# Down projection of a decoder trunk step: residual additions two at a time behind each operand split in VectorE's order, and the splits of a product's last three steps held for its copies

## The chip, the core and the metric

The kernel runs on one core of one Trainium2 chip. The metric is the device time of one execution in microseconds (us). The engines are TensorE (PE in the profile, its weight loads PEld), VectorE (DVE), ScalarE (ACT), GpSimd (POOL) and SyncE (SP), which here issues DMA transfers.

## The reference

One step of a hybrid decoder trunk of one layer: a combined input projection, a gated delta rule, sliding-window attention with sinks, an output projection, and a gated feed-forward block, for 1024 prompt rows and 8 single-token samples. All data is float32. The part that the change touches is the last line of the feed-forward block, the down projection with its gate and residual:

```python
h2 = _rmsnorm(x, lp['norm2_w']) * (1 + sc2) + sh2
gate = h2 @ lp['w_ffn_gate']
up = h2 @ lp['w_ffn_up']
...
gc = _causal_dwconv(gate_ext, lp['ffn_conv_w'], L) + lp['ffn_conv_b']
x = x + gt2 * ((jax.nn.silu(gc) * up) @ lp['w_ffn_down'])
...
y_prompt = _rmsnorm(xp, final_norm_w)
```

Here `w_ffn_down` is 2816 x 1024.

## The kernel before, in words

**Products.** `ffn_down` computes this matrix product as seven products of half-size blocks (a Strassen scheme), named 1 to 7, in the order 5, 3, 4, 7, 1, 2, 6. The inner dimension of each product is taken in G = 11 steps, numbered on through all products: product 5 has the steps 0 to 10, product 3 has 11 to 21, product 4 has 22 to 32, product 7 has 33 to 43, and so on. Products 5 and 3 accumulate in the same eight PSUM banks (a chain), and so do 4 and 7; products 1 and 2 are chains of their own, and product 6 is done behind the loop.

**Operands.** For each step `fetch` loads a block of weights (256 KB) and a block of activations `xd` (258 KB) into a raw buffer. Products 3, 4, 7, 1 and 6 need the sum or the difference of two weight blocks: a second block goes to a buffer `ws`, and GpSimd adds it (L1755). Then `part` splits the raw operand into a high and a low part: ScalarE writes the high part (`hi`, L129), VectorE subtracts it (`lo`, L130). The split operands have 13 rooms (`tags`). The raw buffers are only five: three named `raw` and one, `bmh0`, that holds two steps; a load waits for the split that read its buffer last, five steps earlier.

**Matmuls, copies, additions.** `step` makes 24 matmuls per step: eight banks (p, j), and three (high x high, high x low, low x high; L180 to L182) for each. After a product's eleventh step, `take` has ScalarE copy each bank (L1786) to one of eight slots of `self.copies`. Each copy is put on the list `waiting`, once or twice, as its product belongs to one or two quarters of the output (`home`: two for 5, 3, 1 and 2; one for 4, 7 and 6). `add` takes one off the list and adds it, times the gate, to the residual tiles `x1` on VectorE: one scalar_tensor_tensor (L1472), and for the sample rows two small ones of 8 columns (L1476, L1477). The first homes of all eight copies come before the second homes, so slot 0 is read by the first and by the ninth addition where there are two homes. The next copy into a slot waits for the additions that read it.

**What sets the order.** The order in which each engine gets its instructions is set by a scheduler that plays the program with estimated costs; a semaphore then links what depends on each other. An instruction made inside `issue_after(x)` is placed behind x. `fetch_to(s + 13)` asks, at step s, for loads and splits of up to thirteen steps ahead; with its second argument false it only loads, and the splits are held. `part` puts splits behind the last copy asked for so far (`self.took`). In the kernel before, splits are held in the last six steps of a chain's last product only, and the additions, two per step in the steps 2 to 9 of the next product, are bound by nothing but their operands.

Of the kernel before, what the change touches and what calls it, by code (L numbers as in the profile page):

```python
# [9 lines left out]
F32 = mybir.dt.float32  # L10
# [3 lines left out]
ALU = mybir.AluOpType  # L14
# [50 lines left out]
class Step:  # L65
# [61 lines left out]
    def split(self, hi, lo, x, eng=None):  # L127

        self.nc.scalar.activation(hi, x, AF.Copy)  # L129
        (eng or self.nc.vector).tensor_tensor(lo, x, hi.bitcast(F32), op=ALU.subtract)  # L130

    def load_split(self, pool, shape, src, tags, bufs, raws, home=None, raw=None):

# [1592 lines left out]
    def ffn_down(self, pool, psum):  # L1726

        nc, I = self.nc, self.I
        G, n = FT // 2, NT // 2
        tags = ("bmh2", "bml0", "bml2", "bmh1", "pk2", "bml1", "pk3", "pk6", "pk4", "pk0", "pk5", "pk1", "bmh3")  # L1730
# [7 lines left out]
        ready, loaded, waiting = {}, {}, ([], [])  # L1738
# [3 lines left out]
        def fetch(s):  # L1742
            i, g = steps[s]
            if s % 5 == 3:
                ready["raw"] = self.t(self.bm, [P, KC, QW], "bmh0").rearrange("p k n -> p (k n)")
            raw = self.t(self.pw, [P, n + 512], "raw", bufs=3) if s % 5 < 3 else \
                ready["raw"][:, (s % 5 - 3) * 1040:(s % 5 - 3) * 1040 + n + 512]
            at, *src = made[i]
            src = [x if type(x) is not tuple else
                   I["w_ffn_down"][0][(2 * g + x[0]) * P:(2 * g + x[0] + 1) * P, 512 * x[1]:512 * x[1] + 512] for x in src]  # L1750
            nc.sync.dma_start(raw[:, n:], src[0])
            if len(src) > 1:
                other = self.t(self.pw, [P, 512], "ws", bufs=3)
                nc.sync.dma_start(other, src[1])
                nc.gpsimd.tensor_tensor(raw[:, n:], raw[:, n:], other, op=src[2])  # L1755
            nc.sync.dma_start(raw[:, :n], self.xd[at, g])
            loaded[s] = raw

        def part(s):
            room = self.room(tags[s % len(tags)], [P, KC * QW])  # L1760
            hi, lo = room[:, :n + 512], room[:, n + 512:2 * (n + 512)]
            with ExitStack() as after:
                for ins in (self.last_up, self.last_copy) if 5 <= s < len(tags) else (self.took,) if s >= len(tags) and self.took else ():
                    after.enter_context(self.tc.issue_after(ins.ins))
                self.split(hi, lo, loaded.pop(s))
            ready[s] = hi, lo
            if s == 5:
                less.append(self.t(pool, [P, KC, 9], "less"))
                nc.gpsimd.tensor_scalar(less[0], self.mT[:, 40:48, :], -1.0, None, op0=ALU.mult)
                for j in (2, 3, 4):  # L1770
                    self.x1[j] = self.t(pool, [P, NT], f"x1_{j}")
            if 18 <= s < 24:
                nc.sync.dma_start(self.x1[s - 16], self.x1d[s - 16])

        def step(s, ps, p, j, first, last, kw):
            hi, lo = ready[s]
            x, w = slice(256 * p, 256 * p + 256 + 4 * p), slice(n + j * P, n + j * P + P)
            self.mm3(ps, hi[:, w], lo[:, w], hi[:, x], lo[:, x], first, last, **kw)

        def add(ps, p, j, d, q, sign):  # L1780
            self.add_gated(2 * p + q, ps, j + 4 * d, 40, self.mT[:, 40:48, :] if sign > 0 else less[0])

        def take(ps, i, p, j):
            self.turn = (self.turn + 1) % KC
            r = self.copies[:, self.turn, :256 + 4 * p]
            self.took = nc.scalar.copy(r, ps)  # L1786
            for k, h in enumerate(home[i]):
                waiting[k].append((r, p, j, *h))
# [3 lines left out]
        s = begun = done = 0  # L1792

        def fetch_to(n, split=True):
            nonlocal begun, done
            n = min(n, len(steps))
            while done < n if split else begun < n and begun < done + 4 + (begun % 5 != 3):
                if begun == done or not split:
                    fetch(begun)
                    begun += 1  # L1800
                else:
                    part(done)
                    done += 1

        for c in chains[:-1]:
            ps = {(p, j): self.t(pl, [P, 512], tag, bufs=k)[:, :256 + 4 * p] for (p, j), (pl, tag, k) in zip(order, banks)}
            for i in c:
                for g in range(G):
                    fetch_to(s + len(tags), i != c[-1] or g < G - 6)
                    for p, j in order:  # L1810
                        step(s, ps[p, j], p, j, g == 0 and i == c[0], g == G - 1, {"skip_group_check": True} if i != c[0] else {})
                        if g == G - 1:
                            take(ps[p, j], i, p, j)
                    if g in range(2, 10):
                        for _ in range(2):
                            if waiting[0] or waiting[1]:
                                add(*(waiting[0] or waiting[1]).pop(0))
                    s += 1
        for x in waiting[0] + waiting[1]:
            add(*x)  # L1820
# [251 lines left out]
```

## Time and profile before

| | us |
|---|---|
| three runs | 2094.0, 2088.38, 2085.28 |
| median | 2088.38 |
| profiled execution, span from the first to the last instruction (no other time is given for it) | 2084.4 |
| TensorE busy in it | 2012.7 (97%) |
| VectorE busy | 1347.8 (65%) |
| ScalarE busy | 900.2 (43%) |
| GpSimd busy | 520.2 (25%) |
| mean granted TensorE clock | 0.991 |

The span is 0.9 us under the fastest run and 4.0 under the median. The down projection's TensorE work lies between some 1837 us and the end. A row of a timeline gives the start, the duration, the engine, the line, the operation, and what it writes and reads; the square bracket at its end is the idle time ahead of it on its engine and what ended it. Names are those of the buffers' tags: split operands have names such as pk, bmh and bml, PSUM banks are mm, wv, wy and nr, copies are bml as well (written in L1786, read in L1472), and x is the residual.

### The profile page before, as it was taken

To read this page: it belongs to the slowest core of one execution; us is meant where nothing else is said; L and a number is where in the kernel's file an instruction comes from. 1 tells how busy PE (TensorE), PEld (TensorE's weight loads), DVE (VectorE), ACT (ScalarE), POOL (GpSimd) and SP (SyncE) were. 2 spreads that over 40 slices of the span, in tenths; PEclk is the share of its full clock that TensorE was granted. 3 is DMA by queue.
4 is the path that set the end of the run, shared out by engine and by line. 5 is a ranking of instruction groups with operands and counts; after the bars stand their busy time and mean duration, and the time that the engine had idled before them with its cause. 6 is when DMAs were issued, how large, how long until landed. Compare 5 with 4: busy or idle time off the path is not lost.

```text
span 2084.4 us, 41297 instructions
## 1 busy us (share of the span) xinstructions
PE 2012.7 (97%) x16245; PEld 1910.2 (92%) x16245; DVE 1347.8 (65%) x2714; ACT 900.2 (43%) x2233; POOL 520.2 (25%) x594
## 2 busy tenths in 40 slices
PE   7999998999999999989989999999999999999897
PEld 4987877799999999989989999999999999999897
DVE  5755768473655647656544675578876776767756
ACT  4664545433344243432342542354444444534443
POOL 2000000121321221201111000005575466446421
PEclk9999999999999999999999999999999999999999
DMA  8256443331332322312275855323333333488862
GB/s 300 62 144 210 135 167 116 117 94 51 80 80 61 73 72 52 89 42 62 63 223 172 285 186 163 112 63 97 105 91 112 102 92 112 136 305 266 291 215 94
DMA packets 301887, 275.75 MB, mean 132 GB/s; under 512 B 59730, under 2 KB 248111, under 8 KB 301676
## 3 DMA queue, kind: packets, MB, share of 16 engines
q1 hardware_dynamic: 295642, 252.14, 39.6%
q0 software_dynamic: 5552, 20.37, 2.8%
q8 instruction: 127, 2.08, 0.4%
q14 instruction: 68, 0.56, 0.1%
q10 hardware_dynamic: 498, 0.61, 0.1%
HBM read 212.93 MB, written 62.51 MB: 132 GB/s over the span
## 4 chain that ended last, share of the span: by engine, by line
PE 83%; DVE 5%; DMA 5%; ACT 3%; issue 1%; SPq 1%; POOL 1%; DVEq 0%; POOLq 0%; ACTq 0%
PE mm L180 19%; PE mm L181 18%; PE mm L182 18%; PE wv L180 3%; PE wv L182 3%; PE wv L181 3%; PE wy L182 2%; PE wy L180 2%; PE wy L181 2%; PE pv L652 1%; PE pt L190 1%; PE tp L190 1%; DVE x L1472 1%; PE mm L264 1%; PE rc L954 1%
## 5 line engine op out<-in xcount | busy, mean ns | idle before, releaser
L180 PE MATMUL mm<-b1h,wh 128*128 128x384 f32 (+1 forms) x1520 | 496.9, 328 | 3.7 <-ACT gt L1294 1.6
L181 PE MATMUL mm<-b1l,wh 128*128 128x384 f32 (+1 forms) x1520 | 489.3, 323 | 0.0
L182 PE MATMUL mm<-b1h,wl 128*128 128x384 f32 (+1 forms) x1520 | 488.0, 323 | 0.3 <-DVE wl L130 0.3
L180 PEld LDWEIGHTS mm<-b1h,wh 128*128 128x128 f32 x1520 | 286.7, 189 | 12.4 <-issue 4.6
L181 PEld LDWEIGHTS mm<-b1l,wh 128*128 128x128 f32 x1520 | 287.1, 189 | 4.4 <-issue 3.1
L182 PEld LDWEIGHTS mm<-b1h,wl 128*128 128x128 f32 x1520 | 286.3, 189 | 3.9 <-issue 2.8
L129 ACT ACTIVATE wh<-raw 128x1024 fp32r<-128x1024 f32 x83 | 87.0, 1049 | 122.4 <-PE mm L181 70.2
L130 DVE TENSOR_TENSOR wl<-raw,wh 128x1024 fp32r<-128x1024 f32 x82 | 101.0, 1233 | 57.2 <-ACT wh L129 55.1
L181 PE MATMUL mm<-pk,w 128*128 128x260 f32 (+1 forms) x440 | 124.8, 284 | 1.1 <-DVE pk L130 1.1
L180 PE MATMUL mm<-pk,w 128*128 128x260 f32 (+1 forms) x440 | 124.8, 284 | 0.0
L182 PE MATMUL mm<-pk,w 128*128 128x260 f32 (+1 forms) x440 | 124.5, 283 | 0.0
L130 DVE TENSOR_TENSOR w<-ws,w 128x512 fp32r<-128x512 f32 x88 | 78.0, 886 | 36.9 <-ACT w L129 36.7
L1626 ACT COPY bml<-mm 128x256 f32<-128x256 f32 (+1 forms) x132 | 48.9, 371 | 100.6 <-PE mm L182 96.7
L180 PE MATMUL mm<-bmh,w 128*128 128x260 f32 (+1 forms) x320 | 90.3, 282 | 0.0
L182 PE MATMUL mm<-bmh,w 128*128 128x260 f32 (+1 forms) x320 | 90.1, 282 | 0.0
L1681 DVE SCALAR_TENSOR_TENSOR fa<-fz,fcw,fa 128x512 f32<-128x512 f32 x88 | 75.2, 874 | 18.2 <-ACT fa L1679 17.9
L180 PE MATMUL mm<-b2h,wh 128*128 128x384 f32 (+1 forms) x256 | 83.2, 328 | 2.9 <-ACT wh L129 2.8
L181 PEld LDWEIGHTS mm<-pk,w 128*128 128x128 f32 x440 | 83.2, 189 | 1.3 <-DVE pk L130 1.3
L181 PE MATMUL mm<-b2l,wh 128*128 128x384 f32 (+1 forms) x256 | 83.6, 327 | 0.4 <-DVE b2l L130 0.4
L180 PEld LDWEIGHTS mm<-pk,w 128*128 128x128 f32 x440 | 83.2, 189 | 0.2 <-ACT bml L1626 0.2
L182 PEld LDWEIGHTS mm<-pk,w 128*128 128x128 f32 x440 | 83.4, 190 | 0.0
L182 PE MATMUL mm<-b2h,wl 128*128 128x384 f32 (+1 forms) x256 | 82.8, 326 | 0.0
(645 smaller groups left out, 5886.2 us busy)
## 6 DMA issues: line engine op xcount, KB each, us to landing
raw<-in_w_in_dram SPq DMA_DIRECT2D x59, 512.0 KB
ws<-in_w_ffn_down_dram SPq DMA_DIRECT2D x55, 256.0 KB
raw<-xd SPq DMA_DIRECT2D x47, 258.0 KB
raw<-in_w_ffn_down_dram SPq DMA_DIRECT2D x47, 256.0 KB
raw<-in_w_ffn_gate_dram SPq DMA_DIRECT2D x22, 512.0 KB
raw<-in_w_ffn_up_dram SPq DMA_DIRECT2D x22, 512.0 KB
qst<-in_w_mod_dram SPq DMA_DIRECT2D x16, 512.0 KB
raw<-in_w_mod_dram SPq DMA_DIRECT2D x16, 512.0 KB
```

The costliest lines, as they stand in the source:

```text
L129: self.nc.scalar.activation(hi, x, AF.Copy)
L130: (eng or self.nc.vector).tensor_tensor(lo, x, hi.bitcast(F32), op=ALU.subtract)
L180: mm(ps, whi, xhi, start=first, stop=False, **kw)
L181: mm(ps, whi, xlo, start=False, stop=False, **kw)
L182: self.last_mm = mm(ps, wlo, xhi, start=False, stop=last, **kw).ins
L190: self.nc.tensor.transpose(out, in_, self.ident[:p, :p])
L264: nc.tensor.matmul(ps[32 * j:32 * j + 32], self.cT[:, k0 + j, :], ws[j // 2][:, j % 2, :], start=k0 == 0, stop=k0 > 0)
L652: nc.tensor.matmul(pv[64 * r:64 * r + 64], V[:, n - back, ch], ps[:, r::2, :], start=back == 0, stop=back == (n > 0))
L954: yield step(nc.tensor.matmul(ds, kd[:, n, :], s, start=True, stop=True))
L1472: nc.vector.scalar_tensor_tensor(x[:, :np_], ps[:, :np_], by[:, j, 8:9], x[:, :np_], op0=ALU.mult, op1=ALU.add)
L1626: self.last_copy = nc.scalar.copy(r[p, i], x[p])
L1681: nc.vector.scalar_tensor_tensor(ai[:, c:e], zi[:, j + c:j + e], col(j), ai[:, c:e], op0=ALU.mult, op1=ALU.add)
```

## The change

`split` keeps its VectorE instruction as `self.lo`. In `ffn_down` the splits are now also held in the last three steps of a chain's first product (5 and 4). And the additions of a step, two at most, are placed behind the last split that was asked for, which is that of twelve steps ahead where splits are not held, and otherwise the last one that was not held.

```diff
@@ -127,7 +127,7 @@
     def split(self, hi, lo, x, eng=None):
 
         self.nc.scalar.activation(hi, x, AF.Copy)
-        (eng or self.nc.vector).tensor_tensor(lo, x, hi.bitcast(F32), op=ALU.subtract)
+        self.lo = (eng or self.nc.vector).tensor_tensor(lo, x, hi.bitcast(F32), op=ALU.subtract)
...
@@ -1806,15 +1806,16 @@
             for i in c:
                 for g in range(G):
-                    fetch_to(s + len(tags), i != c[-1] or g < G - 6)
+                    fetch_to(s + len(tags), g < (G - 6 if i == c[-1] else G - 3))
                     for p, j in order:
                         step(s, ps[p, j], p, j, g == 0 and i == c[0], g == G - 1, {"skip_group_check": True} if i != c[0] else {})
                         if g == G - 1:
                             take(ps[p, j], i, p, j)
                     if g in range(2, 10):
-                        for _ in range(2):
-                            if waiting[0] or waiting[1]:
-                                add(*(waiting[0] or waiting[1]).pop(0))
+                        with self.tc.issue_after(self.lo.ins):
+                            for _ in range(2):
+                                if waiting[0] or waiting[1]:
+                                    add(*(waiting[0] or waiting[1]).pop(0))
                     s += 1
```

No instruction is added or removed on any engine; what changes is the order. Lines behind L1815 have a number higher by one in the changed kernel.

VectorE where product 4 takes over from product 3, before. The rows that write bmh_2861, bmh_2864 and bml_2867 are the splits of the steps 25, 26 and 27, and the L1472 rows with `mT` are additions of product 3's copies:

```order
L130 TENSOR_TENSOR bmh_2861_21547<-raw_21541,bmh_2861_21547 128x1028
L130 TENSOR_TENSOR bmh_2864_21582<-raw_21576,bmh_2864_21582 128x1028
L1472 SCALAR_TENSOR_TENSOR x_4_2810_21062<-bml_2334_15602,mT,x_4_2810_21062 128x256 x2
L1472 SCALAR_TENSOR_TENSOR x_4_2810_21062<-bml_2334_15602,mT,x_4_2810_21062 128x260
L1472 SCALAR_TENSOR_TENSOR x_4_2810_21062<-bml_2334_15602,mT,x_4_2810_21062 128x252
L1476 TENSOR_TENSOR gtmp_22120<-bml_2334_15602,mT 128x8
L1472 SCALAR_TENSOR_TENSOR x_5_2785_21012<-bml_2334_15602,mT,x_5_2785_21012 128x256 x2
L1472 SCALAR_TENSOR_TENSOR x_5_2785_21012<-bml_2334_15602,mT,x_5_2785_21012 128x260
L1472 SCALAR_TENSOR_TENSOR x_5_2785_21012<-bml_2334_15602,mT,x_5_2785_21012 128x252
L1476 TENSOR_TENSOR gtmp_22158<-bml_2334_15602,mT 128x8
L1477 TENSOR_TENSOR x_4_2810_21062<-x_4_2810_21062,gtmp_22120 128x8
```

The same place in the changed kernel. The L1472 rows with `less` are additions of product 5's copies, which before stood between the splits of the steps 15 and 18:

```order
L130 TENSOR_TENSOR bmh_2861_21547<-raw_21541,bmh_2861_21547 128x1028
L1472 SCALAR_TENSOR_TENSOR x_0_2332_15597<-bml_2334_15602,less_21058,x_0_2332_15597 128x256
L1472 SCALAR_TENSOR_TENSOR x_0_2332_15597<-bml_2334_15602,less_21058,x_0_2332_15597 128x260
L130 TENSOR_TENSOR bmh_2864_21582<-raw_21576,bmh_2864_21582 128x1028
L1472 SCALAR_TENSOR_TENSOR x_1_2333_15598<-bml_2334_15602,less_21058,x_1_2333_15598 128x256
L1472 SCALAR_TENSOR_TENSOR x_1_2333_15598<-bml_2334_15602,less_21058,x_1_2333_15598 128x260
L130 TENSOR_TENSOR bml_2867_21617<-raw_21611,bml_2867_21617 128x1028
L1472 SCALAR_TENSOR_TENSOR x_2_2808_21060<-bml_2334_15602,less_21058,x_2_2808_21060 128x256
L1472 SCALAR_TENSOR_TENSOR x_2_2808_21060<-bml_2334_15602,less_21058,x_2_2808_21060 128x260
L1472 SCALAR_TENSOR_TENSOR x_3_2809_21061<-bml_2334_15602,less_21058,x_3_2809_21061 128x256
L1472 SCALAR_TENSOR_TENSOR x_3_2809_21061<-bml_2334_15602,less_21058,x_3_2809_21061 128x260
L1472 SCALAR_TENSOR_TENSOR x_4_2810_21062<-bml_2334_15602,less_21058,x_4_2810_21062 128x256
```

Product 5's additions moved from behind its copies to here, two behind each split up to step 27 and the other twelve behind that one; the last row shown, into x_4, is the ninth. Product 3's additions, which stood here, went on to the place shown last.

ScalarE at the same place; bml_2867 is again the split of step 27, and the L1786 rows are the copies of product 3's banks:

```order
 L129 ACTIVATE bmh_2864_21582<-raw_21576 128x1028
+L129 ACTIVATE bml_2867_21617<-raw_21611 128x1028
 L1786 COPY bml_2334_15602<-mm_21015 128x256
 L1786 COPY bml_2334_15602<-wv_21016 128x260
 L1786 COPY bml_2334_15602<-wy_21017 128x256
 L1786 COPY bml_2334_15602<-mm_21018 128x260
-L129 ACTIVATE bml_2867_21617<-raw_21611 128x1028
 L1786 COPY bml_2334_15602<-wv_21019 128x256
+L1786 COPY bml_2334_15602<-mm_21021 128x256
```

Step 27's split moved from the middle of the copies to ahead of them.

VectorE where product 7 takes over from product 4; bmh_2912, bml_2915 and bml_2919 are the splits of the steps 39, 40 and 41, and the L1472 rows are additions of product 3's copies:

```order
 L130 TENSOR_TENSOR bmh_2912_22056<-bmh_2908_22016,bmh_2912_22056 128x1028
+L1472 SCALAR_TENSOR_TENSOR x_7_2787_21014<-bml_2334_15602,mT,x_7_2787_21014 128x256
+L1472 SCALAR_TENSOR_TENSOR x_7_2787_21014<-bml_2334_15602,mT,x_7_2787_21014 128x260
+L130 TENSOR_TENSOR bml_2915_22091<-raw_22085,bml_2915_22091 128x1028
+L1472 SCALAR_TENSOR_TENSOR x_4_2810_21062<-bml_2334_15602,mT,x_4_2810_21062 128x256
+L1472 SCALAR_TENSOR_TENSOR x_4_2810_21062<-bml_2334_15602,mT,x_4_2810_21062 128x252
+L1476 TENSOR_TENSOR gtmp_22120<-bml_2334_15602,mT 128x8
+L1477 TENSOR_TENSOR x_4_2810_21062<-x_4_2810_21062,gtmp_22120 128x8
+L130 TENSOR_TENSOR bml_2919_22129<-raw_22123,bml_2919_22129 128x1028
+L1472 SCALAR_TENSOR_TENSOR x_5_2785_21012<-bml_2334_15602,mT,x_5_2785_21012 128x256
+L1472 SCALAR_TENSOR_TENSOR x_5_2785_21012<-bml_2334_15602,mT,x_5_2785_21012 128x252
+L1476 TENSOR_TENSOR gtmp_22158<-bml_2334_15602,mT 128x8
```

Product 3's additions now stand two behind each split from step 36 on. The ninth, the first into x_4 here, is behind step 40's split, and those into x_5 are behind step 41's. On ScalarE the splits of the steps 40 and 41 likewise moved from among product 4's eight copies and from behind them to ahead of the first.

## The prediction

> **What bounds the kernel now.** I read the page's first part, then TensorE's waits, then stretches of the down projection, then each engine's rows around the two places where one product takes over from another.
>
> ```profile
> PE 2012.7 (97%) x16245; PEld 1910.2 (92%) x16245; DVE 1347.8 (65%) x2714; ACT 900.2 (43%) x2233; POOL 520.2 (25%) x594
> ...
> PE mm L180 <- ACT bml L1786: 5.6, 1, 5.6
> ...
> 1862.00:1894.00 32.00, 32.00 (x271) 32.00 (x270) 25.01 (x34) 13.11 (x18) 18.68 (x11) 1.00 0.91 323
> 1894.00:1934.00 40.00, 34.44 (x288) 34.23 (x287) 33.04 (x38) 17.48 (x25) 21.40 (x15) 0.98 0.83 275
> 1934.00:1962.00 28.00, 28.00 (x215) 28.00 (x216) 22.05 (x27) 12.06 (x16) 15.62 (x10) 0.90 0.88 291
> 1929.37:1932.78 3.41, 0.00 (x0) 0.00 (x0) 1.79 (x2) 0.99 (x2) 1.94 (x2) 1.00 1.02 376
> 1932.78:1936.19 3.41, 2.47 (x11) 2.47 (x12) 2.75 (x2) 3.41 (x10) 2.49 (x2) 0.50 1.03 387
> 1936.19:1939.61 3.42, 3.42 (x18) 3.42 (x17) 3.39 (x6) 2.39 (x4) 1.95 (x2) 0.50 0.94 279
> 1939.61:1943.02 3.41, 3.41 (x31) 3.41 (x30) 3.41 (x6) 1.06 (x1) 1.99 (x2) 1.00 0.88 278
> ```
>
> TensorE is busy for 97% of the span, and in the down projection it waits once, 5.6 us, for a copy that ScalarE makes. The windows give busy time of TensorE, its weight loads, VectorE, ScalarE and GpSimd, then granted clock and DMA share. Only 1894 to 1934 has an idle TensorE; VectorE is busy for 33.0 of its 40 us. After the idle stretch the granted clock is 0.50 for two windows.
>
> ```profile
> 1896.42 0.28 PE L182 MATMUL nr<-pk 128*128 128x260 f32 x1
> 1896.54 0.28 PE L180 MATMUL mm<-pk 128*128 128x256 f32 x1
> ...
> 1927.76 0.28 PE L181 MATMUL nr<-pk 128*128 128x260 f32 x1
> 1927.88 0.28 PE L182 MATMUL nr<-pk 128*128 128x260 f32 x1
> 1933.72 0.58 PE L180 MATMUL mm<-pk 128*128 128x256 f32 x1 [5.56 <-ACT bml L1786]
> ...
> 1934.32 0.41 PE L182 MATMUL mm<-pk 128*128 128x256 f32 x1
> 1934.53 0.41 PE L180 MATMUL mm<-pk 128*128 128x256 f32 x1
> ```
>
> Product 4 starts at 1896.54 with no idle. Product 7 starts at 1933.72 after 5.56 us. Matmuls follow at 0.12 us, and at 0.21 under the halved clock. From 1933.72 to 1939.61 the half clock covers 5.89 us, in which 0.12/0.21 of the work is done: about 2.6 us lost. So the stall of before costs 5.56 + 2.6 = **8.2 us**, and that is all this part of the kernel can give back: 0.39% of the time.
>
> ```profile
> 1910.97 1.21 DVE bmh L130
> ...
> 1912.59 1.31 SPq L1756
> 1913.89 0.05 issue
> 1913.94 4.54 DMA bmh<-in_w_ffn_down_dram
> ...
> 1918.62 1.29 POOL bmh L1755
> 1919.91 0.02 issue
> 1919.93 1.08 ACT pk L129
> 1921.01 0.02 issue
> 1921.04 2.20 DVE pk L130
> ...
> 1933.32 0.36 ACT bml L1786
> 1933.68 0.04 issue
> 1933.72 0.58 PE mm L180
> ```
>
> The chain of waits tells why. Five raw operands fit. Step 34's load goes out when VectorE's split of step 29 frees its room (1910.97), lands 4.54 us later, is summed on GpSimd, split by ScalarE and by VectorE. From there the splits follow each other up to the copy at 1933.32, which stands behind step 39's split on ScalarE.
>
> **The change part by part.** No instruction is added or taken away; three things move. (1) The 16 additions of product 5's copies, and the 16 of product 3's, leave the place right behind the copies; they stand two by two behind the splits of the steps 25 to 27 and 36 to 41. (2) ScalarE's splits of 27, 40 and 41 go ahead of the copies. (3) The splits of 28 to 32 stay behind all eight copies, as before. The eight copy slots link these: a copy may be made only when the additions that read its slot eleven steps earlier are done, and slot 0 is read by the first and the ninth.
>
> ```profile
> L1472 DVE SCALAR_TENSOR_TENSOR x<-bml,mT,x 128x256 f32<-128x256 f32 (+2 forms) x16 | 11.8, 798 | 0.0
> L1472 DVE SCALAR_TENSOR_TENSOR x<-bml,less,x 128x256 f32<-128x256 f32 (+2 forms) x16 | 9.4, 645 | 3.6 <-ACT bml L1786 3.6
> ...
> 1863.21 2.35 DVE L1472 SCALAR_TENSOR_TENSOR x<-bml,less,x 128x256 f32<-128x256 f32 x4 [3.62 <-ACT bml L1786]
> 1865.56 0.87 DVE L1472 SCALAR_TENSOR_TENSOR x<-bml,less,x 128x256 f32<-128x256 f32 x2
> 1891.78 1.23 DVE L130 TENSOR_TENSOR bmh<-raw,bmh 128x1028 fp32r<-128x1028 f32 x1
> 1902.25 1.22 DVE L130 TENSOR_TENSOR bml<-raw,bml 128x1028 fp32r<-128x1028 f32 x1
> 1923.27 6.66 DVE L130 TENSOR_TENSOR pk<-raw,pk 128x1028 fp32r<-128x1028 f32 x3
> 1933.44 1.46 DVE L130 TENSOR_TENSOR bmh<-bmh,bmh 128x1028 fp32r<-128x1028 f32 x1 [2.25 <-ACT bmh L129]
> ...
> 1896.22 1.10 ACT L129 ACTIVATE bml<-raw 128x1028 fp32r<-128x1028 f32 x1
> ...
> 1894.47 1.30 POOL L1755 TENSOR_TENSOR raw<-raw,ws 128x512 f32<-128x512 f32 x1 [0.30 <-DMA ws<-in_w_ffn_down_dram]
> ```
>
> An addition costs 11.8/16 = 0.74 us or 9.4/16 = 0.59 us, and 0.87/2 = 0.43 where GpSimd does not sum beside it. The splits it now follows have a GpSimd sum each, as in the 11.8 row, so I take 0.74; 0.43 and 1.1 (a pair of additions, 0.87, that lets a sum of 1.29 pass first: 2.16/2) are the ends.
>
> The Trainium skill ("SBUF — State Buffer", section "Who interferes with whom") says that a VectorE instruction with both inputs in SBUF and a GpSimd instruction that reads it exclude each other for a whole instruction. The splits of 2.20 us beside sums, against 1.22 alone, agree; taken for every pair of additions it would give 1.1 instead of 0.74 and is one of the rivals below.
>
> *Where product 4 takes over (1896.54).* Product 5's additions were made from 1863.21 on. Now the first two wait for step 25's split, which VectorE made at 1891.78, because only five operands are loaded ahead whatever the order asks. The ninth stands behind step 27's split and four others. Step 27's sum ends at 1894.47 + 1.30 = 1895.8; ScalarE 1.10, VectorE 1.22: 1898.1; five additions of 0.74: 1901.8; the copy and its signal 0.40: 1902.2. That is a new stall of 5.7 us, and by the only stall of that length, 2.6 us of clock: product 4 ends 8.3 us later, at 1928.16 + 8.3 = 1936.5. With 0.43 per addition, and with splits made earlier by the idle 9% of the DMA in 1862 to 1894 (2.9 us), the stall is 1.2 us without a clock loss; the upper end, 1.1 per addition, is 7.5 + 2.6.
>
> *Where product 7 takes over (1933.72).* Here the end is set, since both products are waited for. Seven more additions and eight small ones (0.08 apart) end at 1901.8 + 5.2 + 0.6 = 1907.6; the last copy, 1908.0. Then ScalarE's split of 28, 1.1, and VectorE's of 28 and 29, 1.2 each: 1911.4, where before has 1910.97 + 1.21 = 1912.2. That is 0.8 us earlier, so step 34's split, done at 1921.04 + 2.20 = 1923.2, is done at 1922.4. From there before needs (1934.9 - 1923.2)/5 = 2.33 us per split up to step 39, with VectorE idle for only 2.25 us. Six splits to step 40 are 14.0 us, and the eight additions now among them 5.9; half of the idle, 1.1, hides some: 1922.4 + 14.0 + 5.9 - 1.1 = 1941.2. The ninth addition 0.74, the copy 0.40: TensorE goes on at **1942.3** instead of 1933.72, 5.8 us after product 4's end. In the new order 13 matmuls on two banks stand ahead of the third bank: 2.8 us at half clock, to 1945.1. The third slot's addition stands behind step 41's split: 1941.2 + 1.5 + 0.15 + 2.2 + 0.74 + 0.40 = 1946.2, 1.1 us more. The clock then costs 2.6, as before.
>
> **Sum:** 8.3 for the first stall, 5.8 + 1.1 + 2.6 = 9.5 for the second, less 8.2 that before pays: **+9.6 us**, 2084.4 to 2094.0 of span. The same from the other side: product 7 goes on 1942.3 + 1.1 - 1933.72 = 9.7 later. So the first stall's size hardly matters unless the second goes. At the later takeovers (7 to 1, 1 to 2, 2 to 6) additions also move behind later splits; TensorE does not wait there now, and products 1 and 2 load less (DMA share 0.75, 0.56), so I put nothing on them:
>
> ```profile
> 1962.00:1996.00 34.00, 34.00 (x288) 34.00 (x288) 18.35 (x19) 13.90 (x19) 6.56 (x5) 1.00 0.75 253
> 1996.00:2028.00 32.00, 32.00 (x271) 32.00 (x270) 22.20 (x35) 14.04 (x19) 11.74 (x8) 1.00 0.56 183
> ```
>
> If that cover, VectorE's 15.6 and 9.8 idle us, were gone, a third stall would cost some 5 us. The profiled span is 4.0 us under the median of the runs, 2088.38, so I forecast 2088.4 + 9.6 = **2098.0 us**.
>
> **Rivals.** *Not slower: the additions hide.* What spaces the splits from 34 to 40 may be the loads (DMA share 1.02 and 1.03 in two windows) and not VectorE; then additions cost nothing there. At 0.43 each, the first burst ends 4.5 us before the old one (1898.1 + 12 x 0.43 + 0.6 + 0.4 + 1.1 + 2.4 = 1907.7 against 1912.2). Step 40's split ends at 1923.2 - 4.5 + 14.0 = 1932.7 and TensorE could go on at 1933.5, while product 4, with the first stall at 3.9 + 2.6, ends at 1934.7: no second stall. Net 6.5 - 8.2 = -1.7: 2086.7. It decides once the additions among the splits cost under some 1.5 us together. For it: the DMA share; against it: VectorE's 6.66 us for three splits without a gap.
>
> *The change does what it says.* The copies are no longer late, the bursts no longer delay the loads, both stalls are at most 1.2: 2088.4 - 7.0 = 2081.4. Against it: slot 0 still needs the ninth addition, which now stands behind a split made some 2 us before the copy is due. That the additions stay in place is excluded by the order.
>
> *Every pair meets a sum.* At 1.1 per addition, 12 of the first burst, 8 among the splits and 2 at the end each cost 0.36 more: 7.9, so 2106. For it: the skill's rule and the 2.20 us of the splits; against it: 0.74 is a mean in which sums already stand.
>
> **Chances.** The forecast (2091 to 2102) 0.50, additions hidden 0.18, both stalls gone 0.08, every pair meeting a sum 0.24. About 0.5% (10.4 us) is what a measurement of this kernel can tell from no change: 2078 to 2098.8. The forecast lies just inside, with a little under half of its chance beyond; with the last rival that is 0.47 for slower. The two better rivals fall inside, as 8.2 us is the most that can be had: faster 0.04 (nothing else in the cases gives it), no change 0.49. The range is 2085 to 2107.
>
> **What would show it.** Right: two waits of TensorE for L1786, near 1896.5 (4 to 7 us) and near 1936 (4 to 8 us), half a clock behind each; additions between the L130 rows; copies that wait for VectorE's L1472; split 40 of VectorE ending near 1941. Wrong: no wait near 1896; one of the stalls under 2 us; L130 rows of the steps 34 to 40 still 2.3 us apart with additions between them; or a third stall at products 1, 2 or 6.

## The result, and the profile after

| | before | changed |
|---|---|---|
| median, 6 runs each | 2087.85 us | 2098.66 us |
| range | 2085.28 to 2094.0 | 2093.91 to 2102.0 |
| span of the profiled execution | 2084.4 us | 2093.3 us |
| TensorE idle for copies of the down projection | 5.6 us, one wait | 10.4 us, three waits |

The ratio is 1.0046, with a 95% interval of 1.0031 to 1.0061: the change makes the kernel about 9.6 us slower. The medians lie 10.8 us apart, the profiled spans 8.9.

TensorE's waits in the changed kernel (in all, times, longest), then its rows at the two takeovers and in the last product:

```profile
PE mm L180 <- ACT bml L1786: 10.2, 2, 5.9
...
PE mm L180 <- ACT pk L129: 1.4, 1, 1.4
...
PE wy L180 <- ACT bml L1786: 0.2, 1, 0.2
...
1902.46 0.58 PE L180 MATMUL mm<-pk 128*128 128x256 f32 x1 [5.91 <-ACT bml L1786]
...
1940.99 0.58 PE L180 MATMUL mm<-pk 128*128 128x256 f32 x1 [4.27 <-ACT bml L1786]
...
1946.58 0.39 PE L180 MATMUL wy<-pk 128*128 128x260 f32 x1 [0.22 <-ACT bml L1786]
...
2043.41 0.39 PE L180 MATMUL mm<-pk 128*128 128x260 f32 x1 [1.44 <-ACT pk L129]
```

There are two long waits for L1786, where before had one. Product 4 now starts after 5.91 us of idle time, where it had none; product 7 after 4.27 us, where it had 5.56. A smaller wait in product 6 is new. VectorE and ScalarE at the first takeover:

```profile
1895.90 1.90 DVE L1472 SCALAR_TENSOR_TENSOR x<-bml,less,x 128x256 f32<-128x256 f32 x2
1897.72 1.22 DVE L130 TENSOR_TENSOR bml<-raw,bml 128x1028 fp32r<-128x1028 f32 x1
1898.86 4.47 DVE L1472 SCALAR_TENSOR_TENSOR x<-bml,less,x 128x256 f32<-128x256 f32 x6
...
1894.92 1.07 ACT L129 ACTIVATE bml<-raw 128x1028 fp32r<-128x1028 f32 x1 [0.77 <-POOL raw L1755]
1902.03 0.37 ACT L1786 COPY bml<-mm 128x256 f32<-128x256 f32 x1 [6.05 <-DVE x L1472]
```

Split 27 on VectorE ends at 1898.9, the additions follow, and the first copy starts as the ninth ends: ScalarE waits 6.05 us for L1472. At the second takeover:

```profile
1927.11 1.91 DVE L1472 SCALAR_TENSOR_TENSOR x<-bml,mT,x 128x256 f32<-128x256 f32 x2
1928.94 1.22 DVE L130 TENSOR_TENSOR pk<-raw,pk 128x1028 fp32r<-128x1028 f32 x1
1930.08 1.91 DVE L1472 SCALAR_TENSOR_TENSOR x<-bml,mT,x 128x256 f32<-128x256 f32 x2
1931.91 1.22 DVE L130 TENSOR_TENSOR bmh<-bmh,bmh 128x1028 fp32r<-128x1028 f32 x1
1933.05 2.95 DVE L1472 SCALAR_TENSOR_TENSOR x<-bml,mT,x 128x256 f32<-128x256 f32 x2
1935.92 1.22 DVE L130 TENSOR_TENSOR bmh<-bmh,bmh 128x1028 fp32r<-128x1028 f32 x1
1937.06 1.88 DVE L1472 SCALAR_TENSOR_TENSOR x<-bml,mT,x 128x256 f32<-128x256 f32 x2
1938.86 1.22 DVE L130 TENSOR_TENSOR bml<-raw,bml 128x1028 fp32r<-128x1028 f32 x1
1940.00 0.87 DVE L1472 SCALAR_TENSOR_TENSOR x<-bml,mT,x 128x256 f32<-128x256 f32 x2
...
1940.57 0.37 ACT L1786 COPY bml<-mm 128x256 f32<-128x256 f32 x1 [3.76 <-DVE x L1472]
1942.77 0.37 ACT L1786 COPY bml<-wy 128x256 f32<-128x256 f32 x1 [1.36 <-DVE x L1472]
```

The L130 rows are the splits 37 to 40. Split 40 ends at 1940.1, the ninth addition follows, and then the copy. VectorE has no gap between its rows here. A last place, where product 6 takes over from product 2:

```profile
2031.90 4.54 DVE L1472 SCALAR_TENSOR_TENSOR x<-bml,mT,x 128x256 f32<-128x256 f32 x6
...
2036.15 0.37 ACT L1786 COPY bml<-mm 128x256 f32<-128x256 f32 x1 [7.14 <-PE wv L182]
...
2038.11 0.37 ACT L1786 COPY bml<-wy 128x256 f32<-128x256 f32 x1 [1.10 <-DVE x L1472]
...
2041.47 0.38 ACT L1786 COPY bml<-wy 128x260 f32<-128x260 f32 x1 [2.13 <-DVE gtmp L1476]
...
2042.01 0.40 ACT L1786 COPY bml<-nr 128x260 f32<-128x260 f32 x1
2042.27 1.08 ACT L129 ACTIVATE pk<-raw 128x1028 fp32r<-128x1028 f32 x1
```

Product 1's additions stand behind split 71 and hold the third and the sixth of product 2's copies, for 1.10 and 2.13 us; the first copy waits for TensorE itself. From the first copy to the last it takes 5.9 us, where before took 2.5 (2028.55 to 2031.07), and the splits of product 6 stand behind the last one on ScalarE. TensorE has work from other rows for most of that time and waits 1.44 us.

### The profile page after: what moved, and what is told of

Read it like the earlier page. It is cut to its first block, busy times and chain, and to the rows that moved or that the text cites. A ratio compares the mean times of both kernels' runs of the same rounds, so it can differ in the third digit from the quotient of the medians.

```text
span 2093.3 us, 41296 instructions
## 1 busy us (share of the span) xinstructions
PE 2014.3 (96%) x16245; PEld 1910.3 (91%) x16245; DVE 1357.8 (65%) x2714; ACT 900.2 (43%) x2233; POOL 516.7 (25%) x594
## 4 chain that ended last, share of the span: by engine, by line
PE 77%; DMA 8%; DVE 7%; ACT 3%; issue 2%; SPq 2%; POOL 1%; DVEq 0%; POOLq 0%; ACTq 0%
PE mm L180 17%; PE mm L181 17%; PE mm L182 17%; PE wv L180 2%; PE wv L182 2%; PE wv L181 2%; DVE x L1472 2%; PE wy L180 1%; PE wy L182 1%; PE wy L181 1%; PE pv L652 1%; DMA ws<-in_w_ffn_down_dram 1%; PE pt L190 1%; PE tp L190 1%; PE mm L264 1%
## 5 line engine op out<-in xcount | busy, mean ns | idle before, releaser
L130 DVE TENSOR_TENSOR wl<-raw,wh 128x1024 fp32r<-128x1024 f32 x82 | 101.8, 1242 | 60.5 <-ACT wh L129 59.3
L130 DVE TENSOR_TENSOR w<-ws,w 128x512 fp32r<-128x512 f32 x88 | 78.0, 886 | 37.0 <-ACT w L129 36.9
```

Of the source, the lines that this page charges most:

```text
L130: self.lo = (eng or self.nc.vector).tensor_tensor(lo, x, hi.bitcast(F32), op=ALU.subtract)
```

## The experiments

Three theories: L, late slots: a copy waits for the ninth addition, which the new order ties to a split that VectorE reaches late. H, the hold: splits put ahead of the copies by the new hold make them late. D, load: in products 3 and 4 VectorE and GpSimd have about all the work that TensorE's pace allows, so a stall comes wherever the additions stand. The new hold rule alone leaves the order of VectorE's and ScalarE's splits, copies and additions as in the kernel before, so that kernel was not run.

Executions differ by up to 5 us ahead of the down projection (product 5's first copy lies between 1862.6 and 1867.2 us). So the last column counts the span from that copy on; it and the waits are those of one profiled execution each. The ratios are over runs of the kernel before that were made beside each kernel: its median was 2086.08 us (26 runs) beside the four kernels from "additions alone" to "slot order", and 2086.28 (23 runs) beside the spread ones. "Behind split s+6" means that the additions of step s stand behind the split of step s+6.

| kernel | median us | ratio, 95% interval | waits for L1786 and splits at product 4 / product 7 | span from product 5's first copy |
|---|---|---|---|---|
| before | 2087.85 | | 0 / 5.6 | 221.6 |
| changed | 2098.66 | 1.0046 (1.0031 to 1.0061) | 5.9 / 4.5 | 230.7 |
| additions alone | 2099.14 | 1.0055 (1.0035 to 1.0075) | 6.7 / 5.0 | 233.4 |
| behind split s+6 | 2084.69 | 0.9988 (0.9972 to 1.0003) | 2.5 / 2.1 | 218.4 |
| behind split s+8 | 2087.64 | 1.0005 (0.9990 to 1.0021) | 1.8 / 3.0 | 222.7 |
| slot order | 2090.89 | 1.0019 (1.0005 to 1.0034) | 2.7 / 5.2 | 225.8 |
| before, spread | 2079.54 | 0.9968 (0.9956 to 0.9980) | 0 / 1.4 | 213.3 |
| change, spread | 2088.77 | 1.0014 (0.9999 to 1.0029) | 1.9 / 4.9 | 223.2 |
| before, no sums | 2075.99, one run | | 0 / 0 | 209.5 |
| change, no sums | 2084.16, one run | | 3.9 / 0 | 215.3 |

For the two spread kernels the first figure is at product 4's start, now behind product 2, and the second at product 7's. The wait of 1.44 us at product 6 is not in these figures; additions alone, slot order and the change without sums have it too (1.6, 1.6 and 1.2 us).

**Additions alone.**

```diff
-                    fetch_to(s + len(tags), g < (G - 6 if i == c[-1] else G - 3))
+                    fetch_to(s + len(tags), i != c[-1] or g < G - 6)
```

> Edit: the additions behind the last split that was asked for, as in the change, but the splits held as before (the hold rule undone). Theory L (late slots): the copies wait because the ninth addition stands behind a split that VectorE reaches late; the hold does not matter. L expects both waits of TensorE for L1786 as in the changed kernel (5.9 us at product 4's start, 4.3 at product 7's; here 5 to 7 and 3 to 6) and a time 8 to 13 us above before. Theory H (hold): the splits 27, 40 and 41, put ahead of the copies by the hold, make the copies late. H expects no wait at product 4's start and a time within 3 us of before. Theory D (load): in products 3 and 4 VectorE and GpSimd together have more work than TensorE's 2.87 us per step leaves room for, so a stall comes wherever the additions stand; D expects the same as L here.

```profile
1907.35 0.58 PE L180 MATMUL mm<-pk 128*128 128x256 f32 x1 [6.73 <-ACT bml L1786]
...
1944.99 0.58 PE L180 MATMUL mm<-pk 128*128 128x256 f32 x1 [3.27 <-ACT bml L1786]
```

These are TensorE's rows of that kernel. Both waits are there without the hold, later banks of product 7 wait 1.7 us more, and the time is that of the changed kernel within the intervals. H falls: ScalarE makes split 27 ahead of product 3's copies here too, without the hold, and then waits 6.86 us for the ninth addition. L and D agree here.

**Behind split s+6, and behind split s+8.** The additions of step s are tied to a split that VectorE makes about when TensorE is at step s.

```diff
-                        with self.tc.issue_after(self.lo.ins):
+                        with self.tc.issue_after(los[min(s + 6, max(los))].ins):
```

where `part` keeps each step's VectorE split as `los[s]`; the other kernel has 8 in place of 6.

> Edit: as the change, but the two additions of step s are tied to the split of step s+6 instead of s+12. The ninth addition of product 5 then stands behind split 23 (VectorE made split 25 at 1890.7 in the changed kernel, so 23 before 1889), that of product 3 behind split 35 (made by 1927). L expects no wait at product 4's start, at most 2 us at product 7's, and 6 to 8 us less than before (2080 to 2082). H expects both waits as in the changed kernel. D expects no wait at product 4's start, but still 3 to 6 us at product 7's, since VectorE has the same work: 2086 to 2091.

> Edit: as the change, but the two additions of step s are tied to the split of step s+8. The ninth addition of product 5 stands behind split 25 (ended 1891.9 in the changed kernel), that of product 3 behind split 37. L expects 0 to 2 us at product 4's start, 3 to 6 us at product 7's, and a time between the tie to s+6 and the change (about 2086 to 2092). H expects the waits of the changed kernel (5.9 and 4.3). D expects about the time of the tie to s+6, within 2 us.

TensorE's rows with the tie to s+6:

```profile
1903.17 0.39 PE L181 MATMUL mm<-bmh 128*128 128x256 f32 x1 [2.48 <-DVE bmh L130]
...
1934.18 0.39 PE L180 MATMUL mm<-pk 128*128 128x256 f32 x1 [0.76 <-ACT bml L1786]
1937.84 0.39 PE L180 MATMUL wy<-pk 128*128 128x256 f32 x1 [1.37 <-ACT bml L1786]
```

The time follows the tie: 1.0046 at s+12, 1.0005 at s+8, 0.9988 at s+6. That is L's order. At s+8 both waits and the time lie in L's ranges, and H, which expected 5.9 and 4.3 us in both kernels, falls again. D's ranges did not hold either: 2.1 us at product 7's start with s+6 instead of 3 to 6, and 2.95 us between the two medians instead of at most 2.

But that difference is no longer one of waits: they add up to 4.8 us at s+8 and 4.6 at s+6. From product 5's first copy on the two lie 4.2 us apart, and most of that is the clock, which fell behind product 7's waits at s+8 and stayed at 1.00 at s+6 (last section): the two windows shown there and the next one (clock 0.86) hold 9, 16 and 27 TensorE records in 8.87 us of busy time, and a window of 3.41 us at the full clock holds 30 or 31, so by this estimate about 3 us are lost.

L's 6 to 8 us under before did not come: of the 4.6 us of waits at s+6 the first has a new face, for a split of VectorE itself. VectorE's groups between 1862 and 1934 with the tie to s+6 show why:

```profile
L1472 DVE SCALAR_TENSOR_TENSOR x<-bml,less,x 128x256 f32<-128x256 f32 (+2 forms) x16 | 15.2, 989 | 0.0
L130 DVE TENSOR_TENSOR pk<-raw,pk 128x1028 fp32r<-128x1028 f32 x9 | 13.2, 1463 | 0.0
```

Product 5's 16 additions take 15.2 us, where before, in bursts, they took 9.4. Spread two by two among splits, nearly every pair meets a GpSimd sum: rows such as

```profile
1899.94 1.89 DVE L1472 SCALAR_TENSOR_TENSOR x<-bml,less,x 128x256 f32<-128x256 f32 x2
```

are 1.89 us for a pair that takes 0.87 alone. So spreading costs VectorE 5.8 us more for the same 16 additions; that this is what uses up L's gain is argued, not shown.

**Slot order.** The late ties stay, but both additions of a copy follow each other, so that slot 0 is free after the second.

```diff
-                waiting[k].append((r, p, j, *h))
+                waiting[0].append((r, p, j, *h))
```

> Edit: as the change (ties to the last split asked for, splits held), but the waiting list is in the order of the copies: both additions of a copy follow each other, so slot 0 is free after the second addition, behind split 25, and not after the ninth, behind split 27. L expects the wait at product 4's start to fall from 5.9 us to 0 to 2, that at product 7's from 4.3 to 1 to 3 (the copies of the third and later banks still need additions behind the splits 27 and 38 to 41), and 3 to 8 us less than the changed kernel. H and D expect what the changed kernel shows, 5.9 and 4.3 in all about 10 us of stall, since the splits, their holding and VectorE's work are the same.

ScalarE's rows of that kernel at product 4's start:

```profile
1895.36 0.35 ACT L1786 COPY bml<-mm 128x256 f32<-128x256 f32 x1
...
1899.29 0.38 ACT L1786 COPY bml<-wv 128x260 f32<-128x260 f32 x1 [2.00 <-DVE gtmp L1476]
1902.38 0.37 ACT L1786 COPY bml<-wy 128x256 f32<-128x256 f32 x1 [2.72 <-DVE x L1472]
...
1910.00 0.38 ACT L1786 COPY bml<-nr 128x260 f32<-128x260 f32 x1 [2.82 <-DVE gtmp L1476]
```

The first copy is made at 1895.36 instead of 1902.03, with the same splits, the same additions and the same ties: which slot the additions free first is what held TensorE there. On ScalarE that copy also moved ahead of split 27; but in the changed kernel ScalarE stood idle for 6.05 us behind that split, so it was not the split that held the copy. The later copies come one by one as their additions do. The 5.9 us became 2.7 in three pieces, more than L's 0 to 2; at product 7 the pieces add up to 5.2 us, more than L's 1 to 3. The time, 7.8 us under the changed kernel, is in L's range all the same, and in the profiled executions only 2.5 us of the gain are shorter waits. The windows around product 7's start (columns as in the last section) show the rest:

```profile
1932.78:1936.19 3.41, 1.90 (x16) 1.90 (x17) 3.41 (x4) 1.70 (x3) 2.72 (x3) 1.00 1.02 383
1936.19:1939.61 3.42, 2.18 (x19) 1.97 (x18) 3.42 (x5) 1.33 (x2) 1.90 (x2) 1.00 0.14 51
```

The longest piece is 1.80 us, and the granted clock stays at 1.00, where the changed kernel has half a clock behind each of its two long waits.

**Before, spread, and change, spread.** Product 2, with one weight block per step and no sum, is put between products 3 and 4.

```diff
-        chains = ((5, 3), (4, 7), (1,), (2,), (6,))
+        chains = ((5, 3), (2,), (4, 7), (1,), (6,))
```

> Edit: the kernel before (additions and holds as there), with product 2 between the chains: 5, 3, 2, 4, 7, 1, 6. Product 2 has one weight block per step, so no GpSimd sum and a third less to load, and VectorE can catch up between products 3 and 4. D expects the wait of 5.6 us at product 7's start and the half clock behind it to be gone, and no other over 1 us: 7 to 9 us less than before, 2077 to 2080. L alone, which sees only late slots, expects the wait to stay, as the additions stand where they stood: 2085 to 2089.

> Edit: the changed kernel (ties to the last split asked for, splits held), with product 2 between the chains: 5, 3, 2, 4, 7, 1, 6. L expects the wait at the end of product 3 to stay at 5 to 6 us, as the ninth addition of product 5 is still behind split 27, and another of 2 to 6 us at the end of product 2 or of product 4: 2088 to 2096. D alone expects the sum of these waits to fall under 3 us: 2080 to 2085.

TensorE's waits in the kernel before with this order, then in the changed kernel with it:

```profile
PE mm L180 <- ACT bml L1786: 1.4, 1, 1.4
```

```profile
PE mm L180 <- ACT bml L1786: 5.2, 3, 4.3
...
PE wy L180 <- ACT bml L1786: 1.1, 2, 0.8
PE wv L180 <- ACT bml L1786: 0.5, 1, 0.5
```

Before's 5.6 us fall to 1.4, and the kernel gains 0.32% (0.20 to 0.44%); from the first copy on it is 8.3 us shorter. No tie was added, so the stall of before goes with the load (D) and not with a late tie; D's "gone" and its 7 to 9 us were a little too much, as 1.4 us and 6.7 came. With the change the waits are 6.8 us in this order too, and the kernel is about 9 us slower than the spread one without it; D alone, which expected under 3 us of waits, falls too. L's first wait did not come (none near 1895): I had overlooked that split 27 is then one of product 2, with no sum ahead of it, so the tie to it is not late. The wait moved to product 7's start (4.3 us), where ties to splits with sums stand.

**No sums.** GpSimd's sum of two weight blocks is left out, in the kernel before and in the changed one, so products 3, 4, 7, 1 and 6 are computed with one block of two.

```diff
-                nc.gpsimd.tensor_tensor(raw[:, n:], raw[:, n:], other, op=src[2])
+                pass
```

> Edit: the kernel before without GpSimd's sums of two weight blocks in the down projection (L1755 left out; both blocks are still loaded). Additions and splits of VectorE then have no sum beside them. D expects the wait at product 7's start to be gone, an addition at 0.40 to 0.45 us and all splits at 1.2: a span 7 to 9 us under before, 2076 to 2078. If loads alone spaced the splits, the wait would stay at 4 us or more.

> Edit: the changed kernel without GpSimd's sums of two weight blocks (L1755 left out; both blocks are still loaded). L expects the wait at product 4's start to be smaller, 1 to 3 us instead of 5.9 (split 27 without its sum 1.3 us earlier, five additions of 0.43 instead of 0.9), and the one at product 7's start gone, as VectorE then runs ahead. D expects both gone.

VectorE's group of additions between 1862 and 1934 in the kernel before without sums, then TensorE's and VectorE's rows of the changed one without sums:

```profile
L1472 DVE SCALAR_TENSOR_TENSOR x<-bml,less,x 128x256 f32<-128x256 f32 (+2 forms) x16 | 6.9, 479 | 0.7 <-DMA x<-x1d 0.6
```

```profile
1905.17 0.39 PE L180 MATMUL mm<-pk 128*128 128x256 f32 x1 [3.94 <-ACT bml L1786]
...
1901.42 1.23 DVE L130 TENSOR_TENSOR bml<-raw,bml 128x1028 fp32r<-128x1028 f32 x1 [2.62 <-ACT bml L129]
1902.57 2.46 DVE L1472 SCALAR_TENSOR_TENSOR x<-bml,less,x 128x256 f32<-128x256 f32 x6
```

Without sums the kernel before has no wait at either takeover: D. The changed one keeps 3.94 us at product 4's start, more than L's 1 to 3, with VectorE idle for 2.62 us just ahead of split 27: it was not short of time there, it waited for that operand (ScalarE had waited 3.59 us for its load), and the ninth addition waited behind it. That is the late tie by itself, without sums. The wait at product 7 is gone, as L said.

## Why the prediction was right

The time, 2098.66 against 2098.0, lies in the range, and the mechanism is the one named: late slots at both takeovers, with half a clock behind each. That the time came within 1 us is luck, since misses of some 2 us cancel in it and single runs of the changed kernel lie 8 us apart. Point by point:

- **First stall, new.** Forecast 5.7 us, with TensorE going on at 1902.2; measured 5.91 and 1902.46. Single terms were off and made up for each other: step 27's sum ended at 1894.9 instead of 1895.8, but VectorE made the split 0.8 us later, as the two additions ahead of it took 1.90 us beside a sum. The 16 additions took 11.8 us, 0.74 each as taken. The slot order experiment showed that the ninth addition is the cause, the one without sums that the late tie alone suffices.
- **Its clock loss.** Product 4 ran from 1902.46 to 1936.72 (1940.99 - 4.27), 34.3 us, where before took 31.6: 2.6 lost, as forecast.
- **Second stall.** Forecast: step 40's split done at 1941.2, TensorE on at 1942.3, 1.1 us for the third bank. Measured 1940.1, 1940.99 and 0.22, for the sixth bank. The gain of 0.8 us for step 29's split did not come (1912.3, as before's 1912.2), since the last copy ended at 1908.9 instead of 1908.0. The eight additions among the splits cost more than taken: behind the splits 36 to 39 they took 8.65 us, 1.08 each, not 5.9 (all sixteen, from split 36 on, took 14.2, 0.89 each). The step pace that they were added to was the oversized term: 2.33 us per split came from a stretch with 2.25 us of idle time and with splits of 2.2 us, each beside a sum. With additions in between, the sums fall beside these, and the splits 37 to 40 took 1.22 us each: the forecast counted GpSimd's sums twice. From step 34 to 40 it was 17.4 us with all the additions in it, not 18.8. Product 7 so started 7.3 us later than before, with 0.2 more at a later bank, not 9.7.
- **What was left out.** The later takeovers were priced at nothing, covered by VectorE's idle time; product 6 took a wait of 1.44 us. A third stall there was one of the prediction's own signs of being wrong, and it came. The cover held for products 1 and 2 and was gone at the last, where product 1's and product 2's additions fell together (VectorE busy for 22 of 22 us between 2028 and 2050). The two misses nearly cancel: 8.9 us of span measured, 9.6 forecast.
- **Rivals.** That the additions hide fell: no idle of VectorE was left at product 7. That the change does what it says fell with the two waits. That every pair meets a sum came true for the eight additions that decide the second stall, at 1.08 each, and not for product 5's, at 0.74; but its price supposed that the splits stay as dear as they were, and those among the additions became cheaper (1.22 us for 2.2). With no sums an addition costs 0.43 us (6.9/16), and 0.42 (6.7/16) in the changed kernel. The Trainium skill ("SBUF — State Buffer", section "Who interferes with whom") states that a VectorE instruction with two inputs in SBUF contends with a GpSimd instruction that reads SBUF, and these runs agree.
- **Slips of the working.** The half clock over 5.89 us costs 2.5 us by the prediction's own figures, not 2.6, and the first stall of the first rival is 4.1 us by its own terms, not 3.9. Neither changes the forecast.
- **A point that I had only argued.** The prediction said that the first stall hardly matters unless the second goes. The tie to s+8 and the slot order shorten the first to 1.8 and 2.7 us and are 8 and 5 us faster from the first copy on than the change, so in these two the order of additions moved both; the sentence isn't shown. With the slot order product 7 starts 70.9 us behind product 5's first copy, as in the kernel before, and 78.3 in the changed one.

What stays open: with the tie to s+6 the runs do not separate how much of the 4.6 us of waits that remain is load and how much the dearer additions. For the stall of before, leaving out the sums takes work from VectorE and GpSimd and also shortens each operand's way from its load to its splits, and it lets ScalarE make split 40 ahead of product 4's copies; which of these removes the stall is not separated. Product 2 in between likewise eases the loads as well as the sums.

## What to carry to other kernels

Work that frees a buffer should not be tied to an instruction that is merely issued far ahead: find in the trace when that instruction runs, as here split s+12 was asked for at step s but made about when TensorE was at step s+7 or so, since only five operands could be loaded ahead. When a ring of slots waits, look at which reader of a slot comes last in the order; making a slot's two readers follow each other took 3.2 us of stall away here at one place. And before moving work in time between two engines that block each other, compare its price where it stands with its price where it goes; if a stage is simply too full, try an emptier stage in between: product 2 there (0.9968) did better than every order tried within the stage, though its interval just overlaps that of the tie to s+6 (0.9988).

## What the runs showed of the hardware

The price of an addition on VectorE depends on what GpSimd does beside it. Product 5's 16 additions, the same instruction on the same operands, cost 0.43 us each with no GpSimd sum in the stage, 0.59 in the bursts of the kernel before, 0.74 in the changed one, and 0.95 spread between splits with the tie to s+6.

A wait of TensorE has a price beyond its length, but not always. The changed kernel's windows (busy time of TensorE, its weight loads, VectorE, ScalarE and GpSimd, each with its number of records, then granted clock, DMA share and GB/s) around the first stall, and those of the tie to s+6 around its wait of 2.48 us:

```profile
1898.65:1902.06 3.41, 0.00 (x0) 0.00 (x0) 3.41 (x7) 0.03 (x1) 1.80 (x2) 0.90 1.04 385
1902.06:1905.47 3.41, 3.01 (x14) 3.01 (x15) 3.41 (x4) 1.09 (x3) 3.38 (x3) 0.50 0.64 221
1905.47:1908.90 3.43, 3.43 (x20) 3.43 (x20) 3.05 (x12) 1.75 (x6) 0.56 (x1) 0.60 0.48 153
```

```profile
1898.65:1902.06 3.41, 2.04 (x16) 1.70 (x14) 3.41 (x9) 1.68 (x5) 1.49 (x2) 1.00 1.02 347
1902.06:1905.47 3.41, 2.30 (x19) 2.30 (x19) 3.41 (x6) 1.10 (x4) 2.20 (x1) 1.00 0.90 316
1905.47:1908.90 3.43, 3.43 (x30) 3.37 (x30) 3.24 (x4) 3.01 (x4) 1.95 (x2) 1.00 0.79 277
```

After 5.91 us the clock was near half for two windows; after 2.48 us, split over two windows, it stayed at 1.00. Length alone does not settle it: with the tie to s+8, waits of 1.91 and 0.68 us close together brought the clock down too.

```profile
1936.19:1939.61 3.42, 2.06 (x9) 1.76 (x9) 3.42 (x7) 1.71 (x3) 2.38 (x2) 0.64 0.22 83
1939.61:1943.02 3.41, 3.40 (x16) 3.10 (x16) 3.26 (x6) 2.23 (x4) 0.69 (x1) 0.50 0.76 237
```

In the slot order kernel waits of 1.80, 1.24 and 1.02 us in three such windows left the clock at 1.00. So the idle time of one window does not settle it either (1.36 us here, 1.51 and 1.24 there), and the runs do not show from which idle share on the clock falls.
